# Order of the first head's loads and of the output rows, early halves of x's tile, and three pairs of differences on GpSimd, in an encoder layer on one core

## The chip, the cores and the metric

The kernel runs on one core of a Trainium2 chip. Its engines have their own instruction streams and meet only by semaphores: TensorE (PE, matmuls and transposes), VectorE (DVE), ScalarE (ACT), GpSimd (POOL) and SyncE (SP), which here does nothing but issue DMAs. GpSimd issues DMAs as well. The metric is the device time of one execution in microseconds, lower is better.

## The reference

One layer of a streaming encoder over 1024 prompt frames and 64 sample frames (1088 together, 1024 channels, 8 heads of 64). What the change touches are the attention's bias, the gated merge with its output projection, and the norm ahead of the feed-forward part:

```python
def mixer(xn, ...):
    proj = xn @ w_in
    cb, cc, ch, q, k, v, ga, gb = jnp.split(proj, splits, axis=-1)
    cv, conv_state = causal_conv(cc * ch, conv_prefix, w_conv)
    ya = (cb * cv) @ w_conv_out
    o, new_k, new_v = attn_fn(heads(q), heads(k), heads(v))   # softmax(q k^T / 8 + bias) v in a band
    yb = o.reshape(B, L, ATT_DIM) @ w_attn_out
    merged = jax.nn.sigmoid(ga) * ya + jax.nn.sigmoid(gb) * yb
    return merged @ w_out, conv_state, new_k, new_v

def trunk(x, ...):
    x = x + mixer(rmsnorm(x, g_mix), ...)
    x = x + swiglu(rmsnorm(x, g_ffn), w_ff1, w_ff3, w_ff2)
    return rmsnorm(x, g_final)
```

Everything is float32.

## The kernel before

**Numbers.** A float32 operand of a matmul is kept as two reduced-precision parts: `split` (L126) takes the high part with a cast on ACT (L128) and the low part with a subtraction on DVE (L129). A product is then three matmuls (high by high, high by low, low by high), as in `product` (L336, matmuls at L343 to L345). The two large projections of a norm's output use sums and differences of half blocks, with seven products instead of eight; their operands are called `ax`, `mg` or `xs` (plain quarters) and `tt` (sums and differences), and `run` (L256) issues their matmuls at L277.

**Stages, with their time in the profile.** Loading, the first norm and its transposes to about 64 us; input projections in units of seven products to 385 us (gate a's units store their rows to the scratch tensor `ga_d`, L669); gate b row by row with `product` (L891), beside which attention runs head by head from about 411 to 592 us; the last gate products and the merge loop to 663 us; the output projection token block by token block, with the residual and the second norm, to about 789 us; the up projections to 1224 us and the down projection to the end.

**The order of work.** A scheduler of the language fixes each engine's order when the kernel is built. From then on every engine takes its instructions in that order and stops at one whose semaphores are not there yet, and everything behind it on that engine waits too. SP's DMAs use eight semaphores in turn.

**The first head.** `head_load` (L916) issues a head's loads on SP: q (L921), k (L930 to L932), v (`vd`, `vsd`, L934 to L937) and four pieces of the bias (`bb`, L941 to L944). `scores` (L978) makes the score blocks on PE (L993, L994) and `softmax` (L947) adds the bias and takes the maximum on DVE (L951), then the exponential on ACT (L961). Weight blocks for the gates, called `rawp`, come by `plain_load` (L305, DMA at L309) into two buffers in turn, as soon as DVE has split the block before. Ahead of the first head's loads stand two DMAs (L1131) that bring x's operand back from the scratch tensor `x_d` into a tile that the unit before still used.

**The merge loop.** For output rows m = 0 to 7 of 128 channels, ACT takes a sigmoid (L1177), for m = 6 and 7 DVE multiplies the row of y by its gate a (L1179; the other rows had this earlier), and for each half of the frames PE makes `yb` (three matmuls per contraction block and piece), DVE multiplies by the gate (L1187) and adds (L1188), and `split` writes the merged row to `mg` and, for the last 32 frames of each half, to `ms`. Rows of y and of gate b come by SP (`rows_in`, L1123); four are loaded ahead, and a later one waits until a buffer is free. `wo_half` (L1207) loads the output projection's weights by SP (`wor`, L1211), and `token_product` (L1223) multiplies by them.

**The second norm.** For each block i of 128 tokens the output projection `wo` is added to x (L1247), ACT squares and sums (L1290), a few small instructions make the factor (L183 to L187), DVE scales (`xg`, L1293), and PE transposes eight tiles (L1304). Blocks 0 to 3 and 4 to 7 are combined in pairs, 0 with 4 and so on (column c = 0, 128, 256, 384), and the 64 sample tokens with each other (c = 512, 32 wide). A first block's transpose is kept (`kept`, L1317). When its partner comes, four subtractions on DVE (`minus`, L1332) make the forms: `two_sums` twice, then in `seventh` and `fourth` two differences that overwrite `kept`; each form is split into `tt` or `mg`. For c = 256 and 384 these differences come later, in another place.

Of the kernel before, what the change touches and what calls it, by code (L numbers as in the profile page):

```python
# [8 lines left out]
F32 = mybir.dt.float32  # L9
F32R = mybir.dt.float32r  # L10
AF = mybir.ActivationFunctionType
ALU = mybir.AluOpType
# [3 lines left out]
P = 128  # L16
# [6 lines left out]
HD = 64  # L23
# [43 lines left out]
def encoder_kernel(ctx: ExitStack, tc: tile.TileContext, ins, outs):  # L67
# [281 lines left out]
    for g, m in GATES:  # L349
# [1 line left out]
            base = (C_GA if g == "a" else C_GB) + m * P  # L351
            ld = {"src": w_in[:, base : base + 2 * P], "w": 2 * P}
        plan.append((ld, KD, m % 2 * P))
    for m in range(0, 8, 2):
        ld = {"src": ins["w_attn_out"][0][:, m * P : (m + 2) * P], "w": 2 * P, "at": 40}
        plan += [(ld, 4, j * P) for j in range(2)]

# [463 lines left out]
    def run1(n, unit, ahead):  # L821
        nm, u, _ = units[n]
        return run(unit, ux if nm == "ya" else x7, bank1, snap1, DONE[nm](u), ahead)

    r0 = run1(0, u0, [(u1, {0: (), 1: ()})])
    next(r0)
    next(r0)
# [8 lines left out]
    for n in range(len(units)):  # L836
        if n in (5, 6):
            for j in range(2):
                table_store(2 * (n - 5) + j)
        if n in (4, 5):  # L840
            for j in range(2):
                table_load(2 * (n - 4) + j, slot(STAGE, 768))
        if n == 0:
            r, si = r0, 2
        else:
            if n + 1 < len(units):
                nxt_unit = unit_of(n + 1)
                new = [(nxt_unit, {1: (), 2: (0, 1, 2)} if n == 1 else {})]
            else:
                new = [(PlainNext(), {})]  # L850
            if n == 1:
                ahead += new
                r, si = r1, 2
            else:
                r, si = run1(n, unit, new), 0
            unit = nxt_unit
        if n >= 12 and n < 15:
            gated_load(n - 12)
        if n == 14:
            plain_load(0)  # L860
        for _ in r:
            if n == 12:
                uforms(si)
            if n < 2 and si in (2 + n, 5 + n):
                i = 2 * n + si // 5
                cache_tile(i)
                if i + 2 < 4:
                    cache_load(i + 2)
            if si > 1:
                for f in due:  # L870
                    f()
                due.clear()
            due += late
            late.clear()
            si += 1
# [37 lines left out]
    sm2 = at_pool.tile([P, 2, 9], F32, name="sm2", bufs=1)  # L913
    nc.gpsimd.memset(sm2, 1.0)

    def head_load(h):  # L916
        q = []
        for l in range(2):
            qq = qp.tile([P, T], F32R, tag=f"q{l}", name=f"qd{h}_{l}", bufs=2 + l)
            for j in range(2):  # L920
                nc.sync.dma_start(qq[j * HD : (j + 1) * HD].bitcast(F32), q_d[h, :, l])  # L921
            q.append(qq)
        k = hd_pool.tile([P, TP], F32R, tag="k", name=f"kd{h}")
        ks = hd_pool.tile([P, CACHE + TS], F32R, tag="ks", name=f"ksd{h}", bufs=1)

        for l in range(2):
            ls = slice(l * HD, (l + 1) * HD)
            src = k_d[h, :, l]
            for e in range(2):
                nc.sync.dma_start(k[ls, 512 * e : 512 * e + 512].bitcast(F32), src[:, 576 * e : 576 * e + 512])  # L930
            nc.sync.dma_start(ks[ls, :CACHE].bitcast(F32), src[:, T:])
            nc.sync.dma_start(ks[ls, CACHE:].bitcast(F32), src[:, 512:576])  # L932
        v = hd_pool.tile([P, 8, P], F32R, tag="v", name=f"vd{h}")
        nc.sync.dma_start(v.bitcast(F32), v_d[h, :TP].rearrange("(b p) e -> p b e", p=P))  # L934
        vs = hd_pool.tile([P, 5, P], F32R, tag="vs", name=f"vsd{h}", bufs=1)
        nc.sync.dma_start(vs[:, :4].bitcast(F32), v_d[h, TP : TP + CACHE].rearrange("(b p) e -> p b e", p=P))
        nc.sync.dma_start(vs[:TS, 4].bitcast(F32), v_d[h, TP + CACHE :])  # L937
        b = bb[:, h % 2]
        near = bias_d[h, 127 : 127 + P * 383].rearrange("(p n) -> p n", n=383)
        far = bias_rows(h, 0, 384)  # L940
        nc.sync.dma_start(b[:HD, :384], far[:HD])  # L941
        nc.sync.dma_start(b[HD:, HD:384], far[HD:, HD:])
        nc.sync.dma_start(b[:HD, 384:576], near[:HD, :192])
        nc.sync.dma_start(b[HD:, 384:], near[HD:, :256])  # L944
        heads[h] = (q, k, ks, v, vs, b)

    def softmax(s, ps, bias, sm, nm):  # L947

# [172 lines left out]
    rows = {}  # L1121

    def rows_in(m):  # L1123
        t, z = rows[m] = u_rows.tile([P, T], F32, tag="yg", name=f"yg{m}"), row_tile((m % 5 + 1) % 2, f"gb{m}")
        nc.sync.dma_start(z, gb_d[m * P : (m + 1) * P])
        nc.sync.dma_start(t, y_d[m * P : (m + 1) * P])

    head_load(0)

    for l in range(2):  # L1130
        nc.sync.dma_start(xn.t[0, 1][:, :, l].bitcast(F32), x21_d[:, l])  # L1131
    for i in range(4):
        gate_w[i] = next_w()
        gate(i, (0, 1))
# [6 lines left out]
    for i in range(4, len(GATES)):  # L1141
        gate_w[i] = next_w()
        if i == len(GATES) - LAST:
            for _ in steps:
                pass
            att_stack.close()
            uo = pg_stack.enter_context(tc.tile_pool(name="uo", bufs=1, reuse_waits="tile"))
            uo.tile([P, 48], F32, name="pad_ob")
            t = uo.tile([P, 2, 4 * T + 8], F32R, name="ob")[:, :, : 4 * T]
            ob = Acts(t.rearrange("p l (k t) -> p l k t", k=4))  # L1150
            u_rows = pg_stack.enter_context(tc.tile_pool(name="u_rows", bufs=5, reuse_waits="tile"))
            ga_rows = [uo.tile([P, T], F32, name=f"ga{m}") for m in (6, 7)]
            for k in range(2):
                split(ob.t[:, 0, k], ob.t[:, 1, k], o_rows[k])
            late_r = row_tile(1, "rc2"), row_tile(0, "rc3")
            for k, r in zip((2, 3), late_r):
                o = ob.t[:, 0, k].bitcast(F32)
                nc.sync.dma_start(o, o_d[k * P : (k + 1) * P])
                rc_load(r, k)
                vec.tensor_tensor(r, o, r, op=ALU.mult)  # L1160
                split(ob.t[:, 0, k], ob.t[:, 1, k], r)
            for m in range(4):
                rows_in(m)
        for c in range(4):
            gate(i, (c,))
            between()


    mg = quarters("mg")
    ms = mspool.tile([P, KD, 2, TS], F32R, tag="ms", name="ms")  # L1170
    psum2 = pg_stack.enter_context(tc.tile_pool(name="psum2", bufs=2, space=PSUM, reuse_waits="tile"))
    for m in range(8):
        wb = next_w()
        if m + 4 < 8:
            rows_in(m + 4)
        t, z = rows.pop(m)
        act.activation(z, z, AF.Sigmoid)  # L1177
        if m >= 6:
            vec.tensor_tensor(t, t, ga_rows[m - 6], op=ALU.mult)  # L1179
        for h in range(2):  # L1180
            yb = psum2.tile([P, 2, 512], F32, tag="mm", name=f"yb{m}_{h}")
            for j in range(2):
                product(yb[:, j, :HN], wb, ob, h * HT + j * HN, HN)
            hs = slice(h * HT, (h + 1) * HT)
            zh, th = z[:, hs], t[:, hs]
            two = zh.rearrange("p (j n) -> p j n", j=2)
            vec.tensor_tensor(two, yb[:, :, :HN], two, op=ALU.mult)  # L1187
            vec.tensor_tensor(th, th, zh, op=ALU.add)  # L1188
            split(mg.at(0, m, h * HT, HT), mg.at(1, m, h * HT, HT), th)
            split(ms[:, m, 0, 32 * h : 32 * h + 32], ms[:, m, 1, 32 * h : 32 * h + 32], th[:, 512:])  # L1190
    pg_stack.close()


# [13 lines left out]
    def wo_half(hf):  # L1207
        r = []
        for kq in range(2):
            raw = rpool.tile([P, 4, 512], F32, tag="raw", name=f"wor{hf}_{kq}")  # L1210
            nc.sync.dma_start(  # L1211
                raw,
                ins["w_out"][0][kq * 512 : (kq + 1) * 512, hf * 512 : (hf + 1) * 512].rearrange(
                    "(k p) n -> p k n", p=P
                ),
            )
            for k in range(4):
                hi, lo = moving_pair(f"o{hf}_{kq}_{k}")
                split(hi, lo, raw[:, k])
                r.append((hi, lo))  # L1220
        return r

    def token_product(ps, i, x, kt, w, first=True, last=True):  # L1223

        for k in range(kt):
            wh, wl = w(k)
            f, e = first and k == 0, last and k == kt - 1
            if i < 8:
                mm(ps, x(k, 0), wh, start=f, stop=False)  # L1229
                mm(ps, x(k, 1), wh, start=False, stop=False)  # L1230
# [25 lines left out]
    if True:  # L1256
# [66 lines left out]
        def second_half(src, c, n):  # L1323
# [4 lines left out]
                s = two_sums[:, ORDER.index(8 if c == 512 else c // P + 4) // 2 % 2]  # L1328
            s = s.rearrange("p (a k t) -> p a k t", a=2, k=4)[:, :, :, :n]

            def minus(o, x, y):
                vec.tensor_tensor(o, x, y, op=ALU.subtract)  # L1332

            def seventh():
                minus(f[:, 0], s[:, 1], f[:, 0])
                both(tt[7], c, n, f[:, 0])

            def fifth():
# [2 lines left out]
            def fourth():  # L1341
# [2 lines left out]
                    minus(d, f[:, 1], s[:, 1])  # L1344
                    last_forms.append(lambda: both(ax[0, 1], c, n, d))
                else:
                    minus(f[:, 1], f[:, 1], s[:, 1])
                    both(ax[0, 1], c, n, f[:, 1])

            minus(s[:, 0], src[:, 0], f[:, 0])  # L1350
# [486 lines left out]
```

## Time and profile before

| | us |
|---|---|
| median of 3 runs (1464.27 to 1466.1) | 1464.84 |
| the profiled execution | 1465.99 |
| span of its profile | 1464.2 |
| DVE busy | 996.1 |
| ACT busy | 681.6 |
| POOL busy (DMA issues included) | 144.5 |

PE's granted clock is 0.999 of full speed. In the quoted rows of a timeline stand: start in us from the span's start, duration in us, engine, line, operation, output and inputs, shape, and in square brackets how long the engine had been idle before and what released it. Rows "engine line <- engine line" are waits: total us, times, longest. Rows with a bar are groups: busy us and mean ns of one, then idle time before. A row of a DMA group has the number of DMAs, KB each and the median us from issue to landing.

### The profile page before, as it was taken

Reading aid. Unit: us, or ns where it says so; the run is one execution under the profiler, and the core shown is the slowest. Engines: PE = TensorE matmul, PEld = TensorE weight load, DVE = VectorE, ACT = ScalarE, POOL = GpSimd, SP = SyncE. Lnnn points to the kernel's source line nnn. Section 1 sums busy time; section 2 is a strip of 40 time slices with the busy share of each in tenths; the row PEclk is TensorE's granted clock in tenths of the full one; section 3 lists DMA queues with packets and bytes.
Section 4 is the critical chain, followed back from the end, with each engine's and each line's share of the span. In section 5 each row is a group of like instructions: output and inputs, shape, how many; then the busy total and the mean of one; then the engine's idle time right before and its main releaser. Section 6 shows DMA issues by size and latency. Waiting matters only on the chain.

```text
span 1464.2 us, 26244 instructions
## 1 busy us (share of the span) xinstructions
PE 1447.3 (99%) x10128; PEld 1359.8 (93%) x10128; DVE 996.1 (68%) x1845; ACT 681.6 (47%) x1368; POOL 144.5 (10%) x262
## 2 busy tenths in 40 slices
PE   8999999999999999999999999999999999999997
PEld 6899999999999989998889999999999999888886
DVE  7975475658357677583588667766666668857676
ACT  7654343336357666541455444444344445512223
POOL 1400010001211121000100111111011111000000
PEclk9999999999999999999999999999999999999999
DMA  8686522234787675834432444443334448877685
GB/s 287 183 277 224 177 75 72 67 111 167 254 233 210 175 196 140 290 122 135 158 109 78 162 160 158 151 168 126 123 132 169 148 180 312 281 229 250 208 269 202
DMA packets 157212, 262.47 MB, mean 179 GB/s; under 512 B 18496, under 2 KB 89344, under 8 KB 157088
## 3 DMA queue, kind: packets, MB, share of 16 engines
q1 hardware_dynamic: 134416, 188.53, 40.7%
q0 software_dynamic: 21520, 70.19, 13.4%
q8 instruction: 79, 1.29, 0.4%
q10 hardware_dynamic: 1152, 2.10, 0.4%
q14 instruction: 45, 0.37, 0.1%
HBM read 171.78 MB, written 90.81 MB: 179 GB/s over the span
## 4 chain that ended last, share of the span: by engine, by line
PE 75%; issue 14%; DVE 5%; DMA 3%; ACT 2%; POOL 1%; SPq 0%; POOLq 0%; ACTq 0%; DVEq 0%
PE Ab L277 9%; PE Aa L277 8%; PE A L1750 8%; PE Db L277 4%; PE Da L277 4%; PE D L1750 4%; PE B L1750 2%; PE Bb L277 2%; PE Ba L277 2%; PE wo L1229 2%; PE wo L1231 2%; PE wo L1230 2%; PE t L1040 2%; PE Ak L277 2%; PE Aq L277 2%
## 5 line engine op out<-in xcount | busy, mean ns | idle before, releaser
L343 PE MATMUL g<-xn,wp 128*128 128x272 f32 x320 | 94.0, 294 | 0.0
L344 PE MATMUL g<-xn,wp 128*128 128x272 f32 x320 | 93.2, 291 | 0.0
L345 PE MATMUL g<-xn,low 128*128 128x272 f32 x320 | 92.9, 290 | 0.0
L128 ACT CAST ring<-w2r 128x512 fp32r<-128x512 f32 (+1 forms) x78 | 42.8, 587 | 94.9 <-PE A L1750 50.2
L951 DVE CUSTOM_DVE_ANT_0 p<-s,bb 128x640 f32<-128x640 f32 (+5 forms) x72 | 47.6, 663 | 39.8 <-DMA gb_d<-gst 27.2
L1750 PE MATMUL A<-ring,low 128*128 128x512 f32 x264 | 72.4, 389 | 0.0
L1750 PE MATMUL A<-ring,ht 128*128 128x512 f32 x264 | 72.3, 390 | 0.0
L129 DVE TENSOR_TENSOR low<-rawa,wa 128x512 fp32r<-128x512 f32 x55 | 37.7, 687 | 42.0 <-ACT wa L128 42.0
L343 PEld LDWEIGHTS g<-xn,wp 128*128 128x128 f32 x320 | 60.3, 189 | 0.6
L344 PEld LDWEIGHTS g<-xn,wp 128*128 128x128 f32 x320 | 60.3, 188 | 0.6
L345 PEld LDWEIGHTS g<-xn,low 128*128 128x128 f32 x320 | 60.2, 188 | 0.4
L1750 PEld LDWEIGHTS A<-ring,low 128*128 128x128 f32 x264 | 49.6, 188 | 10.3
L1750 PEld LDWEIGHTS A<-ring,ht 128*128 128x128 f32 x264 | 49.3, 188 | 10.5 <-ACT acc L1760 0.4
L129 DVE TENSOR_TENSOR ring<-w2r,ring 128x512 fp32r<-128x512 f32 (+1 forms) x78 | 48.9, 647 | 14.3 <-ACT ring L128 14.1
L277 PE MATMUL Ab<-tt,wb 128*128 128x272 f32 x352 | 57.8, 285 | 0.4 <-ACT wb L128 0.4
L277 PE MATMUL Ab<-mg,wb 128*128 128x272 f32 x352 | 58.0, 286 | 0.0
L277 PE MATMUL Aa<-mg,wa 128*128 128x272 f32 x352 | 57.7, 285 | 0.0
L277 PE MATMUL Aa<-tt,wa 128*128 128x272 f32 x352 | 57.7, 285 | 0.0
L961 ACT ACTIVATE p<-p,mx 128x640 f32<-128x640 f32 (+5 forms) x72 | 50.8, 706 | 13.5 <-DVE mx L951 13.2
L128 ACT CAST wa<-rawa 128x512 fp32r<-128x512 f32 x55 | 34.0, 621 | 47.1 <-PE Ab L277 33.3
L129 DVE TENSOR_TENSOR pt<-t,pt 128x640 fp32r<-128x640 f32 (+2 forms) x64 | 41.8, 653 | 15.5 <-ACT pt L128 14.7
L128 ACT CAST wb<-rawb 128x512 fp32r<-128x512 f32 x55 | 34.0, 621 | 38.3 <-PE Aa L277 24.5
(583 smaller groups left out, 4504.0 us busy)
## 6 DMA issues: line engine op xcount, KB each, us to landing
h_d<-hq POOLq DMA_DIRECT2D x44, 512.0 KB, 4.2
ht<-h_d SPq DMA_DIRECT2D x77, 256.0 KB, 3.5
low<-h_d SPq DMA_DIRECT2D x77, 256.0 KB, 3.8
h_d<-hq_early POOLq DMA_DIRECT2D x29, 512.0 KB, 4.0
rawa<-in_w_ff SPq DMA_DIRECT2D x11, 1024.0 KB, 5.7
rawb<-in_w_ff SPq DMA_DIRECT2D x11, 1024.0 KB, 5.4
w2r<-in_w_ff SPq DMA_DIRECT2D x11, 1024.0 KB, 7.3
qd<-q_d SPq DMA_DIRECT2D x32, 272.0 KB, 4.1
```

Of the source, the lines that this page charges most:

```text
L128: a = act.copy(hi, src)
L129: b = vec.tensor_tensor(lo, src, hi.bitcast(F32), op=ALU.subtract)
L277: newest[0] = mm(t[:, j, :HN], w[:, k, :], x[p][:, k, l, j * HN : (j + 1) * HN], start=p in (1, 2, 7) and k == 0 and n == 0, stop=k == las ...
L343: mm(out, a, first, start=k == 0, stop=False)
L344: mm(out, a, then, start=False, stop=False)
L345: mm(out, b, p, start=False, stop=k == kt - 1)
L951: vec.tensor_tensor_reduce(out=s if len(ps.shape) == 2 else s.rearrange("p (a b) -> p a b", a=2), in0=ps, in1=bias if len(ps.shape) == 2 e ...
L961: act.activation(s, s, AF.Exp, bias=mx, scale=-1.0, accum_out=sm)
L1040: nc.tensor.transpose(tp[:, i * P : (i + 1) * P], s[:, i * P : (i + 1) * P], ident)
L1229: mm(ps, x(k, 0), wh, start=f, stop=False)
L1230: mm(ps, x(k, 1), wh, start=False, stop=False)
L1750: mm(t, ht[k][:, j, x], w[:, l], start=p in (1, 2, 7) and k == 0 and n == 0, stop=k == len(ks) - 1 and n == 2, skip_group_check=p in (6, 5 ...
```

## The change

Six edits, in the order of the program.

1. Half of x's tile (blocks k = 2 and 3, two DMAs) is loaded during unit 13 rather than ahead of the first head; the other half stays.
2. The first head's bias goes ahead of its v. For the other heads the order stays.
3. The output rows are merged in the order 6, 7, 0 to 5, their weights follow, and the multiplication by gate a of rows 6 and 7 goes into the gate loop.
4. The `ms` pieces of a merged row are made on GpSimd, both halves at once: a cast and a subtraction of 128x64 instead of two casts on ACT and two subtractions on DVE of 128x32.
5. The `wor` loads go from SP's queue to GpSimd's, and `token_product` takes the contraction blocks in the order 0 to 4, 7, 6, 5.
6. In `seventh` and `fourth`, the differences of c = 512, 0 and 128 are taken on GpSimd. Of each pair's four subtractions these are two.

```diff
-    for m in range(0, 8, 2):
+    MERGE = [6, 7, 0, 1, 2, 3, 4, 5]
+    for m in MERGE[::2]:
         ld = {"src": ins["w_attn_out"][0][:, m * P : (m + 2) * P], "w": 2 * P, "at": 40}
...
+    def x21_load(k):
+        for l in range(2):
+            nc.sync.dma_start(xn.t[0, 1][:, k : k + 2, l].bitcast(F32), x21_d[:, l, k : k + 2])
...
         if n >= 12 and n < 15:
             gated_load(n - 12)
+        if n == 13:
+            x21_load(2)
         if n == 14:
             plain_load(0)
...
+        if not h:
+            bias_load(h)
         v = hd_pool.tile([P, 8, P], F32R, tag="v", name=f"vd{h}")
...
-        b = bb[:, h % 2]
...
-        nc.sync.dma_start(b[HD:, 384:], near[HD:, :256])
-        heads[h] = (q, k, ks, v, vs, b)
+        if h:
+            bias_load(h)
+        heads[h] = (q, k, ks, v, vs, bb[:, h % 2])
...
     head_load(0)
 
-    for l in range(2):
-        nc.sync.dma_start(xn.t[0, 1][:, :, l].bitcast(F32), x21_d[:, l])
+    x21_load(0)
...
-            for m in range(4):
+            for m in MERGE[:4]:
                 rows_in(m)
         for c in range(4):
             gate(i, (c,))
             between()
+        if i >= len(GATES) - LAST:
+            m = GATES[i][1]
+            t = rows[m][0]
+            vec.tensor_tensor(t, t, ga_rows[m - 6], op=ALU.mult)
...
-    for m in range(8):
+    for n, m in enumerate(MERGE):
         wb = next_w()
-        if m + 4 < 8:
-            rows_in(m + 4)
+        if n + 4 < 8:
+            rows_in(MERGE[n + 4])
         t, z = rows.pop(m)
         act.activation(z, z, AF.Sigmoid)
-        if m >= 6:
-            vec.tensor_tensor(t, t, ga_rows[m - 6], op=ALU.mult)
+        late = t.rearrange("p (h n) -> p h n", h=2)[:, :, 512:]
+        hi, lo = (ms[:, m, l].rearrange("p (h n) -> p h n", h=2) for l in range(2))
...
-            split(ms[:, m, 0, 32 * h : 32 * h + 32], ms[:, m, 1, 32 * h : 32 * h + 32], th[:, 512:])
+        pool_e.tensor_copy(hi, late)
+        pool_e.tensor_tensor(lo, late, hi.bitcast(F32), op=ALU.subtract)
...
-            nc.sync.dma_start(
+            nc.gpsimd.dma_start(
                 raw,
...
-        for k in range(kt):
+        for k in (0, 1, 2, 3, 4, 7, 6, 5):
...
-            def minus(o, x, y):
-                vec.tensor_tensor(o, x, y, op=ALU.subtract)
+            def minus(o, x, y, on=vec):
+                on.tensor_tensor(o, x, y, op=ALU.subtract)
 
             def seventh():
-                minus(f[:, 0], s[:, 1], f[:, 0])
+                minus(f[:, 0], s[:, 1], f[:, 0], vec if c in (256, 384) else pool_e)
                 both(tt[7], c, n, f[:, 0])
...
-                    minus(f[:, 1], f[:, 1], s[:, 1])
+                    minus(f[:, 1], f[:, 1], s[:, 1], pool_e)
                     both(ax[0, 1], c, n, f[:, 1])
```

What the scheduler makes of it shows in the engines' orders. First SP's around the first head's loads, from x's tile (`xn_99`) on, before:

```order
L1131 DMA xn_99<-x_d 128x4x544 x2
L921 DMA qd_0_4237<-q_d 64x1088 x2
L921 DMA qd_1_4240<-q_d 64x1088 x2
L930 DMA kd_4243<-k_d 64x512 x2
L931 DMA ksd_4244<-k_d 64x512
L932 DMA ksd_4244<-k_d 64x64
L930 DMA kd_4243<-k_d 64x512 x2
L931 DMA ksd_4244<-k_d 64x512
L932 DMA ksd_4244<-k_d 64x64
L934 DMA vd_4253<-v_d 128x8x128
L936 DMA vsd_4255<-v_d 128x4x128
L937 DMA vsd_4255<-v_d 64x128
```

The same place on SP after the change (L937, L946 to L948 are now q and k, L927 and L928 the bias):

```order
L828 DMA xn_99<-x_d 128x2x544 x2
L309 DMA rawp_4656<-in_w_in 128x8x256
L937 DMA qd_0_4239<-q_d 64x1088 x2
L937 DMA qd_1_4242<-q_d 64x1088 x2
L946 DMA kd_4245<-k_d 64x512 x2
L947 DMA ksd_4246<-k_d 64x512
L948 DMA ksd_4246<-k_d 64x64
L946 DMA kd_4245<-k_d 64x512 x2
L947 DMA ksd_4246<-k_d 64x512
L948 DMA ksd_4246<-k_d 64x64
L927 DMA bb<-in_bias_ext 64x384
L928 DMA bb<-in_bias_ext 64x320
```

The x loads are half as large, the bias follows k at once, and a weight block of the gates, which stood behind the first head's loads, now stands ahead of q.

Then DVE in the merge loop, where row 6's y (`yg_7488`) meets its gate a, before:

```order
L1187 TENSOR_TENSOR gb_7115<-yb_1_7524,gb_7115 128x544
L1179 TENSOR_TENSOR yg_7488<-yg_7488,ga_7086 128x1088
L1188 TENSOR_TENSOR yg_7114<-yg_7114,gb_7115 128x544
L129 TENSOR_TENSOR wo_0_1_7925<-wor_0_7920,low 128x512
L1187 TENSOR_TENSOR gb_7119<-yb_0_7565,gb_7119 128x544
L129 TENSOR_TENSOR mg_7337<-yg_7114,mg_7337 128x544
L129 TENSOR_TENSOR ms<-yg_7114,ms 128x32
```

On DVE after the change the two multiplications (now L1182) stand ahead of the loop's first row, among the splits of the gates' last weights:

```order
L1182 TENSOR_TENSOR yg_7108<-yg_7108,ga_7088 128x1088
L129 TENSOR_TENSOR low<-rawp_7415,wp_0_7623 128x512
L129 TENSOR_TENSOR low<-rawp_7553,wp_0_7687 128x512
L129 TENSOR_TENSOR low<-rawp_7553,wp_0_7751 128x512
L1182 TENSOR_TENSOR yg_7112<-yg_7112,ga_7089 128x1088
L1203 TENSOR_TENSOR gb_7109<-yb_0_7355,gb_7109 128x544
L1204 TENSOR_TENSOR yg_7108<-yg_7108,gb_7109 128x544
```

They moved from the middle of the loop to its head, and the `ms` subtractions are gone from DVE's order.

Last the pair c = 0 of the second norm, DVE before, from its first split to the residual behind `xg_2`, the scaled block 2:

```order
L129 TENSOR_TENSOR tt_7914<-two_sums,tt_7914 128x4x128
L1332 TENSOR_TENSOR kept_8382<-two_sums,kept_8382 128x512
L185 RECIPROCAL some<-some 128x1
L129 TENSOR_TENSOR tt_7912<-two_sums,tt_7912 128x4x128
L186 SCALAR_TENSOR_TENSOR some<-some 128x1
L129 TENSOR_TENSOR mg_7338<-xt_4_8479,mg_7338 128x4x128
L187 SCALAR_TENSOR_TENSOR some<-some 128x1
L129 TENSOR_TENSOR tt_7913<-kept_8382,tt_7913 128x4x128
L1293 SCALAR_TENSOR_TENSOR xg_2_8471<-x_2_8441,some,gb_row 128x1024
L1332 TENSOR_TENSOR kept_8382<-kept_8382,two_sums 128x512
L1247 TENSOR_TENSOR x_5_8502<-wo_5_8505,x_5_8502 128x512
L129 TENSOR_TENSOR mg_7337<-kept_8382,mg_7337 128x4x128
```

On DVE after the change, the same stretch (the kept block is now `kept_8368`; L1310 is the scaling, L1264 the residual):

```order
L129 TENSOR_TENSOR tt_7900<-two_sums,tt_7900 128x4x128
L129 TENSOR_TENSOR tt_7898<-two_sums,tt_7898 128x4x128
L185 RECIPROCAL some<-some 128x1
L129 TENSOR_TENSOR mg_7342<-xt_4_8465,mg_7342 128x4x128
L186 SCALAR_TENSOR_TENSOR some<-some 128x1
L129 TENSOR_TENSOR tt_7899<-kept_8368,tt_7899 128x4x128
L187 SCALAR_TENSOR_TENSOR some<-some 128x1
L129 TENSOR_TENSOR mg_7341<-kept_8368,mg_7341 128x4x128
L1310 SCALAR_TENSOR_TENSOR xg_2_8457<-x_2_8427,some,gb_row 128x1024
L1264 TENSOR_TENSOR x_5_8488<-wo_5_8491,x_5_8488 128x512
```

Both differences of `kept` are gone from DVE (GpSimd has them one after the other), and the split of the second one into `mg` moved from behind `xg_2` and the residual of block 5 to a place ahead of `xg_2`.

More of the change, by code (lines that the diff above doesn't have):

```diff
@@ L914, in encoder_kernel, with bias_load @@
     nc.gpsimd.memset(sm2, 1.0)
+    def bias_load(h):
+        b = bb[:, h % 2]
+        near = bias_d[h, 127 : 127 + P * 383].rearrange("(p n) -> p n", n=383)
+        far = bias_rows(h, 0, 384)
+        nc.sync.dma_start(b[:HD, :384], far[:HD])
+        nc.sync.dma_start(b[HD:, HD:384], far[HD:, HD:])
+        nc.sync.dma_start(b[:HD, 384:576], near[:HD, :192])
+        nc.sync.dma_start(b[HD:, 384:], near[HD:, :256])
     def head_load(h):
@@ L937, in head_load @@
         nc.sync.dma_start(vs[:TS, 4].bitcast(F32), v_d[h, TP + CACHE :])
-        b = bb[:, h % 2]
[L939 to L944, printed above, removed]
-        heads[h] = (q, k, ks, v, vs, b)
+        if h:
+            bias_load(h)
+        heads[h] = (q, k, ks, v, vs, bb[:, h % 2])
     def softmax(s, ps, bias, sm, nm):
@@ L1123, in rows_in @@
     def rows_in(m):
-        t, z = rows[m] = u_rows.tile([P, T], F32, tag="yg", name=f"yg{m}"), row_tile((m % 5 + 1) % 2, f"gb{m}")
+        t, z = rows[m] = u_rows.tile([P, T], F32, tag="yg", name=f"yg{m}"), row_tile((MERGE.index(m) % 5 + 1) % 2, f"gb{m}")
         nc.sync.dma_start(z, gb_d[m * P : (m + 1) * P])
@@ L1223, in token_product @@
     def token_product(ps, i, x, kt, w, first=True, last=True):
-        for k in range(kt):
+        for k in (0, 1, 2, 3, 4, 7, 6, 5):
             wh, wl = w(k)
-            f, e = first and k == 0, last and k == kt - 1
+            f, e = first and k == 0, last and k == 5
             if i < 8:
```

## The prediction

> **What bounds the kernel now.** I read the page's busy table first, then the waits grouped by engine, then a window, and last the timeline of each engine around the waits that the change can reach.
>
> ```profile
> PE 1447.3 (99%) x10128; PEld 1359.8 (93%) x10128; DVE 996.1 (68%) x1845; ACT 681.6 (47%) x1368; POOL 144.5 (10%) x262
> 723.00:789.00 66.00, 65.00 (x396) 57.28 (x395) 58.02 (x117) 38.87 (x77) 3.79 (x7) 1.00 0.26 85
> ```
>
> The first row is the page's: PE is busy for 1447.3 us of a span of 1464.2, so some 17 us are idle. The change takes no matmul away, so all it can win is idle time of PE. The second row is the window in which the second norm feeds the transposes (PE, PEld, DVE, ACT, POOL, clock, DMA share, GB/s): PE is busy 65.00 of 66.00 us and DVE 58.02, so DVE sets the pace in places.
>
> ```profile
> PE warm L454 <- ACT ones L452: 2.9, 1, 2.9
> PE s L993 <- DVE mx L951: 1.3, 2, 1.0
> PE t L1040 <- DVE pt L129: 1.2, 5, 0.5
> PE yb L343 <- DVE gb L1187: 1.0, 1, 1.0
> ...
> PE xt L1304 <- DVE xg L1293: 0.6, 1, 0.6
> PE Ab L277 <- ACT wb L128: 0.4, 1, 0.4
> ```
>
> These are PE's waits (total us, times, longest) without two at the start, as `warm` is, which the change leaves alone. Within reach are the long `s` wait, `yb`, `xt` and `Ab`: 1.0 + 1.0 + 0.6 + 0.4 = 3.0 us, with the 1.2 us of `t` as a fringe. A measurement of this kernel can tell about 0.2% from no change, which is 2.93 us. So nearly all of it would have to go for a clear gain. A wait costs a little more than its idle time:
>
> ```profile
> 643.41 0.29 PE L344 MATMUL yb<-ob,wp 128*128 128x272 f32 x1
> 643.53 0.29 PE L345 MATMUL yb<-ob,low 128*128 128x272 f32 x1
> 644.85 0.39 PE L343 MATMUL yb<-ob,wp 128*128 128x272 f32 x1 [1.03 <-DVE gb L1187]
> ```
>
> Matmuls of this form start 0.12 us apart (643.41 to 643.53). Here 1.32 lie between two starts, so 1.20 is lost where 1.03 is idle. I add the difference, 0.17, to each wait that goes.
>
> **The change part by part, first head.** PE stands before the third score block of the first head:
>
> ```profile
> 413.59 0.45 PE L993 MATMUL s<-kd,qd 128*128 128x384 f32 x1 [1.02 <-DVE mx L951]
> 413.23 0.29 DVE L951 CUSTOM_DVE_ANT_0 p<-s,bb 128x128 f32<-128x128 f32 x1 [27.19 <-DMA gb_d<-gst]
> 405.04 0.53 SPq L934 DMA_DIRECT2D vd<-v_d  x1
> 406.80 0.59 SPq L941 DMA_DIRECT2D bb<-in_bias_ext  x1
> 408.72 0.59 SPq L944 DMA_DIRECT2D bb<-bias_d  x1
> bb<-bias_d SPq DMA_DIRECT2D x1, 64.0 KB, 4.3
> xn<-x_d SPq DMA_DIRECT2D x2, 1088.0 KB, 13.0
> ```
>
> DVE begins the first softmax at 413.23. The releaser named, an output of the gates, has nothing to do with this instruction; what its operands need last is the bias tile `bb`, whose fourth load goes out at 408.72 and lands 4.3 us later, at 413.0. The scores were there by about 412.0. The change puts the four bias loads ahead of the three loads of `vd` and `vsd`, which take SP from 405.04 to 406.80. So the bias lands 1.76 us earlier, at 411.3, and DVE can start as soon as the scores are there. The wait goes: 1.02 + 0.17 = **1.19 us**.
>
> The other part decides whether these times hold. Half of x's tile goes out some 40 us earlier, which takes 1.1 MB out of the queue ahead of the first head. But a weight block (`rawp`, 128x8x256 floats, 1.0 MB) now stands in the place of that half. In all some 2.1 MB stand ahead of the first `qd` load, before and after. I count no gain from the early half, and no loss: the two x loads (2 x 1088 KB, 13.0 us to landing) show a queue that was full anyhow.
>
> The early half has a price at its new place, among the stores of `ga_d`. These must land before their row tiles are used again:
>
> ```profile
> 347.90 0.61 ACT L264 COPY scr<-Aya 128x544 f32<-128x544 f32 x1
> 349.12 0.66 PE L277 MATMUL Aya<-xs,wya 128*128 128x272 f32 x4
> ```
>
> The copy empties a PSUM bank into such a tile, with 0.61 us to spare before PE's next group (348.51 to 349.12). Two loads of some 544 KB share the queue with stores that land in 3 to 4 us; stores that are 1.2 us later would cost PE 0.6, and none costs nothing. I take the middle, **0.3 us lost**.
>
> **The merge.** The `yb` wait above has its cause nine us earlier, on DVE:
>
> ```profile
> 633.77 1.29 DVE L1179 TENSOR_TENSOR yg<-yg,ga 128x1088 f32<-128x1088 f32 x1 [1.32 <-DMA yg<-y_d]
> 637.69 0.32 SPq L1126 DMA_DIRECT2D yg<-y_d  x1
> 642.13 1.29 DVE L1179 TENSOR_TENSOR yg<-yg,ga 128x1088 f32<-128x1088 f32 x1 [0.42 <-DMA yg<-y_d]
> ```
>
> These two multiplications belong to rows 6 and 7, needed only some 15 us later, yet they stand in DVE's order ahead of work that PE waits for, and wait themselves for 1.32 and 0.42 us for loads that had to wait for a free slot (the second was issued at 637.69). With rows 6 and 7 first, both are done in the gate loop, where nothing waits behind them but two weight splits; the loads that come late are now those of rows 2 to 5, with four rows' work (4 x 5.9 us, by 48 matmuls of 0.12 each) ahead of them. Also 16 small subtractions leave DVE (0.18 each, 2.9 us). The 16 instructions that go to GpSimd, and the `wor` loads on its queue, stand behind nobody that PE needs soon: `ms` is read last in the contraction. The wait goes: 1.03 + 0.17 = **1.20 us**.
>
> **The differences on GpSimd.** Three pairs of subtractions go (one pair 128x4x32, two 128x512), of 0.69 us each at full width:
>
> ```profile
> 740.75 0.69 DVE L1332 TENSOR_TENSOR two_sums<-xt,two_sums 128x512 f32<-128x512 f32 x1
> 744.90 1.28 DVE L1293 SCALAR_TENSOR_TENSOR xg<-x,some,gb_row 128x1024 f32<-128x1024 f32 x1
> L1304 PE MATMUL xt<-ident,xg x40: 270/273/331, 746.3 to 773.5; 128*128 128x128 f32 x40
> 753.99 0.69 DVE L1332 TENSOR_TENSOR two_sums<-xt,two_sums 128x512 f32<-128x512 f32 x1
> 759.04 0.49 PE L1304 MATMUL xt<-ident,xg 128*128 128x128 f32 x3
> ```
>
> In the new order DVE's `mg<-kept` stands ahead of the next `xg`, and it needs both differences and a cast on ACT. With P the time of one difference on GpSimd, the chain at the first full pair is: sums end at 741.44, two differences 2P, cast 0.62, subtraction 0.69, `xg` 1.28, some 0.3 for four handoffs, so `xg` ends at 744.33 + 2P. Today it ends at 746.18, and PE's transposes start 0.15 later (746.3, the first start in the third row). From **P = 0.96** on, PE waits. At the second pair: 754.68 + 2P + 2.89 against PE at 759.04 plus one `wo` matmul (0.22) that moves ahead, less up to 0.35 that the row block before comes earlier.
>
> No row shows a difference on GpSimd. What there is:
>
> ```profile
> L911 POOL MEMSET bb<- 64x64 f32 x2 | 0.3, 146 | 0.1
> masks.py:199 POOL TENSOR_SCALAR_AFFINE_SELECT ident<-ident 128x128 f32<-128x128 f32 x1 | 0.3, 288 | 0.1
> L1828 POOL MEMSET const-float32-1.0<- 128x1 f32 x1 | 0.1, 103 | 0.0
> ```
>
> The low end is DVE's 0.69. From the select, 0.10 fixed and 0.185 for 128 columns give 0.84 for 512; the memset stretched whole (0.146 x 8) gives 1.17 as the high end. A difference reads two operands where the select reads one, so I take P = 1.0. That costs 0.1 at the first pair and 0 to 0.4 at the second: **0.3 us lost** in all.
>
> In return comes the `xt` wait, at the row block behind the second pair:
>
> ```profile
> 760.81 0.62 ACT L128 CAST wa<-rawa 128x512 fp32r<-128x512 f32 x1 [0.29 <-PE wo L1231]
> 761.34 1.06 ACT L1290 ACTIVATE xg<-x 128x1024 f32<-128x1024 f32 x1
> 765.98 0.77 PE L1304 MATMUL xt<-ident,xg 128*128 128x128 f32 x5 [0.58 <-DVE xg L1293]
> ```
>
> The square at 761.34 starts the chain that ends in this `xg`. It stands behind a weight cast at 760.81, which the new order puts later, and its input comes right behind `xg` of the block before. So it starts some 1.1 us earlier, more than the 0.58: 0.58 + 0.17 = **0.75 us won**.
>
> The last wait, `Ab`, hangs on DVE too:
>
> ```profile
> 787.26 0.69 DVE L228 TENSOR_TENSOR sf<-sf,rawb 128x512 f32<-128x512 f32 x1
> 788.65 0.77 PE L277 MATMUL Ab<-tt,wb 128*128 128x272 f32 x4 [0.41 <-ACT wb L128]
> ```
>
> DVE is all but continuous from 764 to here. It starts that stretch about 1.1 us earlier, but two weight splits that stood before it (0.6 each) are now in it, and PE arrives 0.58 earlier. I leave it as it is (0 to 0.7).
>
> The sum: 1.19 + 1.20 + 0.75 - 0.3 - 0.3 = 2.54 us. The profiled execution took 1465.99, 1.15 above the median of 1464.84 and inside the runs shown (1464.27 to 1466.1). The waits are taken to be the same in all, so I subtract from the median: **1462.3 us**.
>
> [...]
>
> **The rivals.**
> *All of it goes.* If P is under 0.9, the pairs cost nothing, and if DVE's earlier start outlasts the two splits, `Ab` goes too (0.41 + 0.17), and the stores cost nothing: 2.54 + 0.3 + 0.3 + 0.58 = 3.7 us, 1461.1. For it speaks that GpSimd is nearly idle here (3.79 of 66 us); against it that DVE is full up to `Ab`.
> *The bias still comes late.* The weight block waits for a split on DVE; if it enters the queue late, everything behind it shifts. From 0.7 us of shift on (bias at 411.3, needed at 412.0) the first wait comes back: 1.2 less, 1463.5.
> *Slower: GpSimd and DVE hold each other off.* If the two engines can't run side by side, each difference waits for a DVE instruction under way (0.69), and P is in effect 1.7 or more, at both pairs. Each 0.1 of P costs 0.2 per pair, 0.4 in all. At P = 1.7 the loss is 4 x 0.74 = 3.0 at the pairs instead of 0.3, and the sum is a gain of 2.84 - 3.0, nothing. That is the point from which it turns; at P = 2.0 it is 1.3 us slower, 1466.2, and at 2.4 some 2.9, 1467.8. For it speaks that DVE is busy 58.02 of 66 us here and has few gaps into which GpSimd would fit; against it that nothing in this profile shows one engine slowed by the other.
>
> **How the numbers follow.** The forecast (gain 1.8 to 2.9) has 0.43; all goes 0.32; the bias late 0.10; GpSimd slow 0.15. Over 2.93 us of gain come only from the second, and a piece of the first's upper edge: faster 0.36. The third, most of the first, and over half of the last lie within 0.2%: 0.55. Slower takes P beyond 2.4, with a little for `t` waits that grow: 0.09. The range goes from 1460.4, where half of the `t` waits goes too, to 1467.0, with GpSimd at P = 2.2.
>
> **What would show it.** After the change: no `s` wait near 412 and the first softmax right after the scores; no `yb` wait in the merge; GpSimd's 128x512 subtractions with their own duration, 1.0 or otherwise, and whether DVE's 0.69 ones grow beside them; `xg` of the row blocks 2 and 3 against their transposes; the `xt` wait gone, `Ab` still there. I am wrong if a difference takes over 1.2 us, if DVE's instructions stretch, or if new `t` waits come from the loads' new order in the attention.

## The result, and the profile after

| | before | changed |
|---|---|---|
| median of 6 runs each, us | 1465.28 (1464.27 to 1466.1) | 1472.09 (1470.38 to 1473.99) |
| ratio, 95% interval | 1 | 1.0045 (1.0035 to 1.0055) |
| profiled execution / span, us | 1465.99 / 1464.2 | 1471.39 / 1469.5 |

The change makes the kernel slower by 0.45%, 6.8 us between the medians, where 2.5 us of gain were forecast (1462.3, with a range from 1460.4 to 1467.0). PE's waits in the changed kernel (total us, times, longest):

```profile
PE xt L1321 <- DVE xg L1310: 4.3, 2, 2.2
...
PE yb L343 <- ACT ob L128: 1.0, 1, 1.0
PE g L343 <- ACT ga L905: 0.9, 1, 0.9
PE t L1053 <- DVE pt L129: 0.7, 4, 0.2
PE wo L1248 <- DVE wo L129: 0.7, 1, 0.7
...
PE s L1006 <- DVE mx L964: 0.3, 1, 0.3
```

The long `s` wait and the `yb` wait for `gb` are gone, as forecast. The `xt` waits, which were to go, now take 4.3 us, and three waits are new: the first `yb` (now for a cast of `ob`), a gate piece `g` behind it, and the first `wo` product: 1.0 + 0.9 + 0.7 = 2.6 us.

The windows of the second norm in the changed kernel (PE, PEld, DVE, ACT, POOL busy, granted clock, DMA share, GB/s) show a second loss:

```profile
723.00:789.00 66.00, 61.72 (x358) 53.53 (x357) 54.12 (x104) 34.77 (x71) 10.73 (x13) 0.97 0.26 88
762.00:764.00 2.00, 0.36 (x2) 0.00 (x0) 2.00 (x4) 0.62 (x1) 0.00 (x0) 1.00 0.00 0
764.00:766.00 2.00, 1.47 (x9) 1.47 (x10) 0.98 (x2) 0.98 (x2) 0.56 (x1) 0.80 0.25 67
766.00:768.00 2.00, 2.00 (x6) 1.55 (x5) 0.88 (x5) 2.00 (x6) 0.00 (x0) 0.50 0.91 321
```

PE is busy 61.72 of 66 us (65.00 before). And behind the second `xt` wait its granted clock falls to 0.50; behind the first it stays at 1.00. The timeline of PE there:

```profile
764.53 1.31 PE L1321 MATMUL xt<-ident,xg 128*128 128x128 f32 x8 [2.17 <-DVE xg L1310]
...
766.06 0.63 PE L1248 MATMUL wo<-wo,mg 128*128 128x512 f32 x1
766.49 0.63 PE L1246 MATMUL wo<-low,mg 128*128 128x512 f32 x1
```

These matmuls start 0.43 us apart, where they start 0.23 apart otherwise. Seven pitches are long, six by 0.20 and the first by 0.35: 1.55 us.

What happens at the first pair shows in GpSimd's timeline:

```profile
742.45 1.29 POOL L1349 TENSOR_TENSOR kept<-two_sums,kept 128x512 f32<-128x512 f32 x1 [0.90 <-ACT xg L1307]
743.69 1.74 POOL L1349 TENSOR_TENSOR kept<-kept,two_sums 128x512 f32<-128x512 f32 x1
```

beside DVE's, where "x2" puts two instructions into one row:

```profile
742.49 3.49 DVE L129 TENSOR_TENSOR tt<-two_sums,tt 128x512 fp32r<-128x512 f32 x2
747.97 1.27 DVE L1310 SCALAR_TENSOR_TENSOR xg<-x,some,gb_row 128x1024 f32<-128x1024 f32 x1
```

and PE's, which waits for the last of them:

```profile
749.38 0.85 PE L1321 MATMUL xt<-ident,xg 128*128 128x128 f32 x6 [2.11 <-DVE xg L1310]
```

While GpSimd takes its two differences, DVE's two subtractions last 3.49 us together. In the kernel before the same two took 0.69 and 0.67:

```profile
741.62 0.69 DVE L129 TENSOR_TENSOR tt<-two_sums,tt 128x512 fp32r<-128x512 f32 x1
742.91 0.67 DVE L129 TENSOR_TENSOR tt<-two_sums,tt 128x512 fp32r<-128x512 f32 x1
```

Now each took 1.8 (1.77 and 1.79 by the view of their tile): the first begins 0.04 behind GpSimd's first and ends 0.5 after it; GpSimd's second, begun meanwhile, ends at 745.43, and DVE's second ends 0.55 later. So the two engines take turns, one whole instruction at a time. The first two had both begun, at 742.45 and 742.49, so this is no wait for a semaphore: these two engines don't meet by semaphores alone.

### The profile page after: what moved, and what is told of

The parts are those of the page before. It is cut to its first block, busy times and chain, and to the rows that moved or that the text cites. A ratio compares the mean times of both kernels' runs of the same rounds, so it can differ in the third digit from the quotient of the medians.

```text
span 1469.5 us, 26241 instructions
## 1 busy us (share of the span) xinstructions
PE 1449.9 (99%) x10128; PEld 1361.5 (93%) x10128; DVE 995.7 (68%) x1823; ACT 681.3 (46%) x1352; POOL 161.9 (11%) x288
## 3 DMA queue, kind: packets, MB, share of 16 engines
q8 instruction: 79, 1.29, 0.4%
## 4 chain that ended last, share of the span: by engine, by line
PE 51%; DVE 3%; ACT 1%; issue 0%; ACTq 0%
PE Ab L277 9%; PE Aa L277 8%; PE A L1767 8%; PE Db L277 4%; PE Da L277 4%; PE D L1767 4%; PE Ba L277 2%; PE B L1767 2%; PE Bb L277 2%; PE wo L1248 2%; PE wo L1246 2%; PE wo L1247 2%; PE ys L1594 2%; DVE tt L129 1%; PE xt L1321 0%; DVE mg L129 0%
```

## The experiments

Each of the first four kernels changes one thing, to find which edit made the loss. Each ratio is to runs of the kernel before beside it, whose medians were 1464.6 to 1464.93. The early half of x's tile (edit 1), the `ms` work on GpSimd (edit 4) and edit 5 were not run alone.

**Differences back on DVE**, all other edits kept.

```diff
-                minus(f[:, 0], s[:, 1], f[:, 0], vec if c in (256, 384) else pool_e)
+                minus(f[:, 0], s[:, 1], f[:, 0])
...
-                    minus(f[:, 1], f[:, 1], s[:, 1], pool_e)
+                    minus(f[:, 1], f[:, 1], s[:, 1])
```

> The changed kernel with the six differences back on VectorE, all else as changed. Blocking theory (the two differences on GpSimd hold VectorE's subtractions up, PE waits 2.1 us twice and then runs slowly for some 3 us): both long xt waits go and PE's granted clock stays at 1.00 in that window, the old 0.6 us xt wait may come back; 4.6 us of waits and 1.6 us of clock less, 0.6 more: about 1466.5 us, 1 us above the kernel before, since the new waits at the merge (1.0, 0.9 and 0.7 us) stay. Rival, the other five edits made the loss: it stays at 1470 or more.

Measured: 1465.55 us, ratio to the kernel before 1.0004 (0.9996 to 1.0013). The window of the second norm, in the columns above:

```profile
723.00:789.00 66.00, 65.31 (x398) 57.25 (x397) 57.99 (x119) 38.72 (x78) 3.79 (x7) 1.00 0.25 88
```

and PE's waits at the merge:

```profile
PE g L343 <- ACT ga L905: 0.9, 1, 0.9
...
PE yb L343 <- ACT ob L128: 0.5, 1, 0.5
PE wo L1248 <- DVE wo L129: 0.5, 1, 0.5
```

That is 0.9 us less than expected: clock and busy share are back, and no `xt` wait is listed at all, not even the old one of 0.6. Two things follow: the differences make the loss, and the other five edits together bring no gain that can be told from nothing.

**Differences alone** on the kernel before (the edit above the other way).

> The kernel before with only the six differences on GpSimd. Blocking theory: both xt waits of about 2.1 us appear, the wait at the row block behind them and part of the Ab wait go: 4.6 - 0.75 - 0.35 + 1.6 of clock = 5 us above the kernel before, about 1470, with VectorE's 128x512 subtractions at 1.8 us beside GpSimd's instead of 0.69. Rival, the loss came from the other edits: within 1 us of the kernel before.

Measured: 1470.27 us, ratio 1.0035 (1.0022 to 1.0048); two `xt` waits (3.6 us in all, the longest 2.1), as expected. At the first pair DVE's two subtractions take 3.50 us together, and PE waits 2.1. At the second pair DVE's first is no later than GpSimd's (both start at 759.43): it takes its usual 0.69, GpSimd's first takes 1.85, and of DVE's two only the second is stretched, 2.40 together; PE waits 1.5. So in these rows the cost of a pair goes with which engine begins first.

The clock is at 1.00 in every window of the norm, so the 1.6 us for the clock didn't come in that execution. It was still the slowest of the six (1466.67 to 1472.8): from the first input projection's first product (`Aq`) to the first `yb` it took 533.0 us, where the kernel before took 530.1, in work that the edit leaves alone.

**Rows in the new order alone** on the kernel before: the edits of `MERGE` and of the multiplication in the gate loop, as in the diff above.

> The kernel before with only the output rows in the order 6, 7, 0 to 5 and the two gate multiplications in the gate loop. Theory of the late row (row 6's gate b is the last but one to be made; its load lands late, the sigmoid that waits for it stands at the head of ACT's order ahead of the casts of ob): the yb wait at 644 goes (1.2 us), waits before the first yb and the next gate piece come (2.0 us): about 0.8 us above the kernel before, 1466. Rival, the late load in the changed kernel came from the new order of the head's loads or the wor loads on GpSimd: no such waits, 1.2 us below, 1464.

Measured: 1465.34 us, ratio 1.0003 (0.9994 to 1.0011). The `yb` wait is gone, a wait of 0.5 us before a gate piece has come, behind a first sigmoid that waits 1.84 us for its gate b; 2.0 us of new waits were expected. The size of 0.8 us can't be told from nothing with this interval, but the gain of 1.2 is not there.

**Bias ahead of v alone** on the kernel before.

```diff
+        if not h:
+            bias_load(h)
         v = hd_pool.tile([P, 8, P], F32R, tag="v", name=f"vd{h}")
...
+        if h:
+            bias_load(h)
```

> The kernel before with only the first head's bias ahead of its v. Theory: bias lands 1.8 us earlier, the 1.0 us wait of PE before the third score block goes, 1.2 us below the kernel before, about 1464.1. Rival, the wait went in the changed kernel only because x's tile was halved ahead of the head's loads: the wait stays and the time is within 0.3 us of the kernel before.

Measured: 1465.26 us, ratio 1.0007 (0.9998 to 1.0015). The long `s` wait is gone and no time is won. Why: see the kernel before, profiled again, below.

**Rows in the order 0, 1, 6, 7, 2 to 5**, on the changed kernel with the differences on DVE:

```diff
-    MERGE = [6, 7, 0, 1, 2, 3, 4, 5]
+    MERGE = [0, 1, 6, 7, 2, 3, 4, 5]
```

> The changed kernel with the six differences back on VectorE and the output rows in the order 0, 1, 6, 7, 2 to 5. Theory of the late row: with row 0 first the first sigmoid no longer waits for a late load, so the waits before the first yb and the next gate piece (0.5 and 0.9 us in the run with the differences back) go, while rows 6 and 7 still have their gate multiplication ahead of the loop: 1.4 us less than that run, about 1464.1, 0.5 us below the kernel before. Rival, the casts of ob are late for another reason (the new head order, the loads on GpSimd's queue): the waits stay, 1465.5.

The reason for this run is ACT's timeline in the changed kernel:

```profile
594.48 1.28 ACT L1193 ACT_TABLE_LOAD   x1 [3.44 <-DMA gb<-gb_d]
596.79 1.08 ACT L128 CAST ob<-o 128x1088 fp32r<-128x1088 f32 x1
```

beside ACT's timeline in the kernel before:

```profile
590.62 1.28 ACT L1177 ACT_TABLE_LOAD   x1
593.02 2.10 ACT L128 CAST ob<-o 128x1088 fp32r<-128x1088 f32 x2
```

The sigmoid of the loop's first row, with its table load, stands ahead of the casts of `ob` on ACT. In the changed kernel it waits 3.44 us for row 6's gate b, and the casts come 3.8 us later. Measured with row 0 first: 1463.84 us, ratio 0.9990 (0.9981 to 1.0000); the waits before `yb`, `g` and also the one before `wo` are gone, 1.7 us less than with rows 6 and 7 first. There the first sigmoid waits for no load, and the casts of `ob` begin at 592.29. So the late row is shown.

**The same, with the `wor` loads back on SP.**

```diff
-            nc.gpsimd.dma_start(
+            nc.sync.dma_start(
                 raw,
```

> As the run before it (rows 0, 1, 6, 7, 2 to 5, differences on VectorE), with the wor loads back on SyncE's queue. Theory: the 0.5 us wait of PE at the first wo product comes from a weight load that stands behind the ms work on GpSimd's queue; it goes, 0.5 us less than with the loads on GpSimd, about 1463.6. Rival, that wait comes from VectorE's own order at the end of the merge loop: it stays, and the time with it.

Measured: 1463.46 us, ratio 0.9988 (0.9979 to 0.9998), 1.5 us below the kernel before and the lowest median of all; the 0.4 us to the run before it can't be told from nothing. Neither theory of the `wo` wait held: it was gone already in the run before, with the loads on GpSimd. The late first row alone doesn't make it either, for the run with the new row order alone, with its loads on SP, has no `wo` wait; what makes it stays open. PE's waits that are left, without those at the start:

```profile
PE t L1053 <- DVE pt L129: 0.7, 4, 0.2
PE Ab L277 <- ACT wb L128: 0.6, 1, 0.6
PE s L1006 <- DVE mx L964: 0.3, 1, 0.3
PE A L1767 <- ACT acc L1777: 0.2, 1, 0.2
```

**Only the second difference on GpSimd**, on the kernel before: the edit in `fourth` alone.

> The kernel before with only the second difference of each pair (the one of fourth) on GpSimd. Nothing ahead of xg waits for it in the order of this kernel. Blocking theory: GpSimd's 1.25 us still hold VectorE's next two-input subtraction up, that one lasts 1.8 us, xg of blocks 2 and 3 comes 1.1 us late, PE waits 1.0 and 0.8 us there, the old 0.6 us wait goes: about 1.2 us above the kernel before, 1465.8, and with waits of 1 us PE's clock stays at 1.00 in that window. Rival, the loss is only the length of the chain through two slow differences: no wait at blocks 2 and 3, VectorE's subtractions at 0.69, 0.6 us below the kernel before.

Measured: 1467.81 us, ratio 1.0020 (1.0011 to 1.0029). GpSimd's group of the whole span:

```profile
L1332 POOL TENSOR_TENSOR kept<-kept,two_sums 128x512 f32<-128x512 f32 x2 | 3.0, 1494 | 1.7 <-ACT tt L128 0.9 <-DVE some L183 0.8
```

DVE's group in the window of the two pairs:

```profile
L129 DVE TENSOR_TENSOR tt<-two_sums,tt 128x512 fp32r<-128x512 f32 x4 | 4.9, 1214 | 0.1
```

and PE's waits there:

```profile
PE xt L1304 <- DVE xg L1293: 1.7, 2, 1.0
PE Ab L277 <- DVE mg L129: 0.6, 1, 0.6
```

Nothing ahead of `xg` needs this difference, and still `xg` is late: one of DVE's two `tt` subtractions at each pair is stretched (a mean of 1.21 over four is two at 0.68 and two at 1.75). So it is the blocking, not the length of the chain. It cost more than expected (2.9 us over the kernel before, not 1.2), since one more wait came at `Ab` (0.6) and the old one there grew from 0.4 to 0.8. The clock stayed at 1.00 in every window of the norm.

**A probe** on the kernel before: GpSimd works for nobody, with a subtraction behind each of eight residuals, and a 128x1 copy and two memsets at the two pairs.

```diff
             residual(i, ps, xt, 512, f"o0_{i}")
+            if i < 8:
+                pool_e.tensor_tensor(probe, xt, xt, op=ALU.subtract)
...
             minus(s[:, 1], src[:, 1], s[:, 0])
+            if c in (0, 128):
+                pool_e.tensor_copy(probe[:, :1], s[:, 1, 0, :1])
+                pool_e.memset(probe, 0.0)
+                pool_e.memset(probe, 0.0)
```

> The kernel before with extra work on GpSimd whose output nobody reads: eight 128x512 subtractions in the first half of the output projection, where VectorE is mostly idle, and at the pairs c = 0 and 128 two 128x512 memsets each, which only write, beside VectorE's subtractions. Blocking theory: a subtraction alone takes 1.2 to 1.3 us, so 1.75 held a wait for VectorE; the memsets, which read nothing, leave VectorE's subtractions at 0.69, and PE has no new wait. Rival 1, a subtraction takes 1.75 by itself: it shows 1.75 here. Rival 2, any work on GpSimd slows VectorE: its subtractions are stretched beside the memsets.

Measured: 1465.19 us, ratio 1.0004 (0.9994 to 1.0015). Groups of GpSimd in the whole span:

```profile
L1271 POOL TENSOR_TENSOR probe<-xr 128x512 f32<-128x512 f32 x8 | 8.6, 1070 | 93.1 <-DVE xr L1247 93.1
L1357 POOL MEMSET probe<- 128x512 f32 x2 | 1.1, 530 | 0.1
```

and of DVE in the window of the two pairs:

```profile
L129 DVE TENSOR_TENSOR tt<-two_sums,tt 128x512 fp32r<-128x512 f32 x4 | 2.7, 681 | 0.1
```

A subtraction takes 1.07 us in the mean (1.2 to 1.3 was expected). Seven of the eight take 1.03 or 1.04; the other met a DVE subtraction under way (`wo<-wor,low`) and took 1.34. These two share no tile, so it isn't two readers of one tile that hold each other up. The memsets, which read no tile, left DVE's subtractions at 0.68. Rivals 1 and 2 fall, and PE has no new wait in the norm.

That DVE's inputs matter too shows in the changed kernel's merge loop. DVE's timeline:

```profile
636.20 0.73 DVE L129 TENSOR_TENSOR mg<-yg,mg 128x544 fp32r<-128x544 f32 x1
...
649.55 0.72 DVE L1203 TENSOR_TENSOR gb<-yb,gb 128x544 f32<-128x544 f32 x1
```

and GpSimd's, with its `ms` work beside them:

```profile
636.27 0.84 POOL L1207 TENSOR_TENSOR ms<-yg,ms 128x64 fp32r<-128x64 f32 x1
...
649.81 0.32 POOL L1207 TENSOR_TENSOR ms<-yg,ms 128x64 fp32r<-128x64 f32 x1
```

The same small subtraction on GpSimd takes 0.32 us beside a DVE multiplication that has one input in PSUM (`yb`, which PE wrote), and 0.84 beside a DVE subtraction with both inputs in SBUF: it ends only behind that one's end (637.11 against 636.93).

These rows and those above show three parts of how the two hold each other up. GpSimd was held up beside two SBUF inputs on DVE and not beside one (0.84 against 0.32). DVE was held up beside a GpSimd instruction that reads and not beside one that only writes (1.8 against 0.68). And the wait was for a whole instruction: at the first pair each of DVE's two subtractions ends 0.5 to 0.55 us behind the end of GpSimd's that it met.

**The changed kernel and the kernel before once more**, for second profiles, with no edit.

> The changed kernel once more, for a second profile. Blocking theory: the two long xt waits (2.1 and 2.2 us) and VectorE's subtractions of 1.8 us come again, since only the order and GpSimd's durations make them; the half clock behind the second wait (0.50 for some 3 us in the first profile) may or may not, since the six runs of the changed kernel spread by 3.6 us with mean clocks from 0.995 to 0.999. Rival: the waits are an accident of one execution and differ by more than 0.5 us.

The profiled execution ran at a mean granted clock of 0.753 and took 1775.33 us; the other took 1470.35. With PE that much slower no `xt` wait is listed, so whether the two waits come again stays open. What DVE and GpSimd do to each other does come again: GpSimd's four 128x512 differences take 1.63 to 1.74 us. DVE begins first at both pairs, and its two subtractions take 2.38 together, as at the second pair of the differences alone.

> The kernel before once more, for a second profile. Theory that the wait for the first head's bias is an accident of loads: the s wait is 0.3 us here, as in four profiles of kernels with the old order of the head's loads, and the yb, xt and Ab waits (0.8 to 1.0, 0.6, 0.4) come again. Rival, the wait belongs to the order: 1.0 us again.

Measured: 1465.34 us; waits `s` 0.3, `xt` 0.6, `Ab` 0.4, and `yb` 0.3, where 0.8 to 1.0 was expected. The first head in SP's timeline:

```profile
408.00 0.59 SPq L944 DMA_DIRECT2D bb<-bias_d  x1
```

and in DVE's:

```profile
412.75 0.29 DVE L951 CUSTOM_DVE_ANT_0 p<-s,bb 128x128 f32<-128x128 f32 x1 [26.23 <-PE s L994]
```

The last bias load goes out 0.7 us earlier than in the first profile and lands 3.0 us later, not 4.3, and DVE's first softmax waits for the scores, not for the bias. With this order of the loads five more profiles (differences alone, rows alone, second difference, probe, and this one) all have 0.3 us. The 1.0 us of the first profile came with when the loads landed in that execution, not with the order.

**One pair on GpSimd**: the changed kernel with the differences of c = 128 back on DVE.

```diff
-                minus(f[:, 0], s[:, 1], f[:, 0], vec if c in (256, 384) else pool_e)
+                minus(f[:, 0], s[:, 1], f[:, 0], vec if c in (128, 256, 384) else pool_e)
...
-                    minus(f[:, 1], f[:, 1], s[:, 1], pool_e)
+                    minus(f[:, 1], f[:, 1], s[:, 1], vec if c == 128 else pool_e)
```

> The changed kernel with the differences of c = 128 back on VectorE, those of c = 0 and 512 on GpSimd. Blocking theory, each pair pays for itself: one xt wait of 2.1 us at block 2, none at block 3, the wait behind it stays away or comes back with 0.6: 2.3 us above the run with all differences on VectorE (1465.55), so 1467.5 to 1468.5, and the granted clock stays at 1.00, if it takes the second long wait to bring it down. Rival, the loss is made at the end of the norm by all pairs together: under 1466.5.

Measured: 1468.97 us, ratio 1.0025 (1.0013 to 1.0036), 3.4 us above the run with all on DVE. PE's one `xt` wait:

```profile
PE xt L1321 <- DVE xg L1310: 2.1, 1, 2.1
```

and the window behind it, in the columns above:

```profile
750.00:756.00 6.00, 6.00 (x28) 4.93 (x27) 3.64 (x7) 1.71 (x4) 0.00 (x0) 0.82 0.41 142
```

From 750 to 752 us the clock is 0.50. Each pair pays for itself: 3.4 us for one, 6.5 for two (1472.09 against 1465.55). But the clock fell behind this single wait, so the guess that it takes the second one was wrong.

## Why the prediction failed

- **First head, 1.19 us.** The wait was read rightly (the bias came after the scores) and the order does move the bias ahead; the wait went to 0.3. What failed is that one profiled execution was taken for all: with the old order five other profiles have 0.3 too. Worth of the edit: none that can be measured.
- **Early half of x's tile, 0.3 us lost.** No such wait is in the changed kernel's list, so no loss shows.
- **The merge, 1.20 us.** The two multiplications did stand in the way, and with them gone the wait was gone. The step looked only at what rows 6 and 7 need on DVE. It didn't look at ACT, where the loop's first sigmoid stands ahead of the casts of `ob`; with row 6 first it waits for a gate row that lands 4 us later. Waits came back at other places: 2.6 us in the changed kernel's profile with the one before `wo`, 1.9 with the differences back on DVE, 0.5 with the row order alone. With rows 0 and 1 first both the old wait and these are gone. The old wait's size was also uncertain: 0.3 in the second profile of before.
- **Time of a difference, 1.0 us.** Right for GpSimd alone: 1.03 or 1.04 in seven of the probe's eight subtractions.
- **What a difference does to DVE, 0.3 us lost.** Here the sum failed: 4.6 us were lost at the two pairs. It took `xg` to come by the path through GpSimd (both differences, a cast, a subtraction), 2P + 2.89, with DVE's instructions at their old durations. That path didn't set the time. In the changed kernel GpSimd's second difference ends at 745.43 and its cast at 746.09, but DVE takes up `mg<-kept` only at 747.37:

```profile
745.47 0.62 ACT L128 CAST mg<-kept 128x512 fp32r<-128x512 f32 x1 [1.08 <-POOL kept L1349]
747.37 0.68 DVE L129 TENSOR_TENSOR mg<-kept,mg 128x512 fp32r<-128x512 f32 x1
```

  DVE's own order set it, with subtractions of 1.8 us in place of 0.69. From the end of the sums to the start of `xg` it takes 3.46 us in the kernel before (741.44 to 744.90), 4.56 with the second difference alone (743.57 to 748.13) and 5.66 in the changed kernel (742.31 to 747.97): 1.10 more for each stretched subtraction. (In the changed kernel one difference less and one split more stand in this stretch, some 0.6 us each.) The forecast's chain would need P = 2.02 for the measured 6.93 us to the end of `xg` (749.24); that fits the number and not the path. That DVE's instructions stretch was among the prediction's own signs of being wrong.
- **The rival "hold each other off".** It had the cause, two engines that can't run side by side, but priced it as GpSimd waiting for DVE and not DVE for GpSimd. At P = 2.0 its price is 4 x 1.04 = 4.2 us for the two pairs; PE's starts at the two waits lie 2.50 and 2.57 us apart where 0.22 to 0.23 is usual, so 4.6 were lost there. That these are close is in part luck. It had a chance of 0.15, and its total of 1466.2 set against it the gains of the first head, the merge and the `xt` wait, and left out the clock.
- **The `xt` wait behind the second pair, 0.75 us.** It is gone, but also in the kernel with the differences on DVE, so it was not for GpSimd to win. With the row order alone and with the bias alone it is still 0.6, and with the `wor` loads back on SP it stays away. That leaves the early half, the `ms` work and the order of the contraction blocks, or some of them together; none was tried alone.
- **The clock.** Not in the sum: 1.55 us in the profiled execution.

Together, in the profiled executions: 4.3 - 0.6 at `xt`, 1.55 of clock and 2.6 of new waits, less 1.0 at the old `yb` wait, 1.0 at `s`, 0.5 at `t` and 0.4 at `Ab`: 3.7 + 1.55 + 2.6 - 2.9 = 4.95 us of the 5.3 by which the spans differ (1469.5 - 1464.2), waits at the start left out. With five such waits come and four gone, one restart more (0.17) makes half of the rest. The medians differ by 6.8; where the other 1.5 us lie, these two profiles don't show.

## What to carry to other kernels

An idle engine is no free place if its reads and the busy one's hold each other up: price work moved from DVE to GpSimd as if both ran on one engine (at the first pair four instructions took 3.5 us, about their sum), unless DVE's instructions beside it are like the multiplication with one of its two inputs in PSUM (GpSimd's subtraction stayed at 0.32 us) or GpSimd's are like the memsets, which only write (DVE's stayed at 0.68). Before a wait of about a microsecond is bought off, look at it in a second profile; an accident of DMA landings reads like a dependency (the `s` wait, 1.0 us in one profile with the old order and 0.3 in five others). When rows are reordered, ask for each engine what the new first row waits for and what stands behind it.

## What the runs showed of the hardware that was not expected

- GpSimd and DVE held each other up by whole instructions, where DVE's had two SBUF inputs and GpSimd's read: 0.69 us became 1.8 on DVE, 1.03 became 1.29 to 1.85 on GpSimd. The one that began first went first: GpSimd's at the first pair of the changed kernel (742.45 against 742.49, and DVE's first took 1.77), DVE's at the second pair of the differences alone (it took 0.69, GpSimd's first 1.85). Why GpSimd's takes 1.29 even then isn't explained by this. Four such instructions took 3.5 us, where GpSimd's two alone need 2.06 and DVE's two 1.38: the sum.
- A PE wait of 2.1 to 2.2 us can be followed by about 3 us at half the clock (0.50): behind the changed kernel's second wait (2.17) and behind that of one pair (2.1). Behind the changed kernel's first wait (2.11) and those of the differences alone (2.1 and 1.5) it didn't come, nor behind waits up to 1.0. What decides it wasn't found.
- What makes the spread of runs stays open. Of the ten runs of one pair (1464.64 to 1472.04), the five with a mean clock of 0.996 or 0.997 took 1468.8 us or more, the other five 1469.13 or less. But one stretch at half the clock cost 1.55 us, and the slowest run of the differences alone (1472.8) has 0.999, so the clock goes with the spread without accounting for all of it.
